# Keeping the small matmuls of side work together, in front of the products of the next step

## The chip, the core and the metric

The kernel runs on one core of a Trainium2 chip. The metric is the device time of one execution in microseconds (us). The engines are named as in the profile: PE is TensorE (PEld its weight loads), DVE is VectorE, ACT is ScalarE, POOL is GpSimd, and SP issues most of the DMAs.

## The reference

Sequence length T = 256, model width D = 1024, batch 1, float32. Two blocks follow each other, each with two layers. Cut to its core:

```
for l in range(2):                                   # first block
    h = rms_norm(x);  z = h @ w_in + b_in
    ya = dilated_mixture_attention(rope(aq), rope(ak), av)      # 8 heads of 64
    qk = silu(causal_short_conv(z[q, k]))                       # 4 taps
    hm = mlstm_chunkwise(mq, mk, mv, mi, mf)                    # 4 heads of 128
    x += (sig(ga) * (ya @ w_proj_att) + sig(gb) * (yb @ w_proj_mlstm)) @ w_out
    x += relu(rms_norm(x) @ w_ff1) ** 2 @ w_ff2                 # 4096 wide
x = rms_norm(x)
for l in range(2):                                   # second block
    x += 0.5 * rms_norm(swiglu(rms_norm(x)))                    # 2816 wide
    z = rms_norm(x) @ w_in
    branches = gmlp(uv), pool(pz), sparse_attention(q, k, v, index), conv(cz)   # 256 wide each
    y = sum(sigmoid(gate_n) * (branch_n @ w_branch[n]) for n in range(4))
    x += rms_norm(y @ w_out)
    x += 0.5 * rms_norm(swiglu(rms_norm(x)))
```

The gMLP mixes tokens with a causal 128x128 matrix per group. Pool takes window means of 2 to 16 tokens. Sparse attention lets each query see the 64 keys that an index score picks. Conv is a depthwise convolution of 31 taps.

## The kernel before

All large matrix products are made of three TensorE products: each operand is split into a high part and a low part, and high x high, high x low and low x high are added in PSUM. Weights are streamed once, about 1 MB a tile: SP loads a tile (RAWS = 3 raw buffers), ACT casts the high part (L214), DVE subtracts to get the low part (L223); five high and four low tiles are held.

The work is written as a list of steps (`prog`). A step is one function of one weight tile. The products of a step are `a_mm` (tokens on the output's partitions; L309, L310 and L313; 512 or 256 columns) and `w_mm` (features on partitions; L322 to L324; 256 columns; a `w_step` has 48 of them). The ten phases are mix, ff, mix, ff of the first block, then f1, mix, f2, f1, mix, f2 of the second. At the border of two phases (`seam`), the two halves of the tokens are staggered, so that the norm of one goes on under the products of the other.

Everything else in the mixing phases is **side work**: generators that are put on a list by `spawn`. After each step `tick` advances every generator on the list by one piece (up to its next `yield`). The pieces that issue TensorE work are `prep` (rotary embedding and transposes of q and k), `gates_chain` (the stabiliser of the mLSTM; L865 to L867), `attend` (L768, L792), `mlstm` (L880, L881, L897), `gmlp` (L1106), `pool` (L1126 to L1135), `conv`, `choose` (L1202, the index score), `sparse` (L1231, L1254), `go` and, once at the start, `toeplitz` (L419). Transposes are recorded at L327. `choose` is spawned by the step that computes the index queries and keys, whose results ACT first copies out (L1268, L1270, L1272).

The program text is only one input to the order on the engines. A scheduler at build time plays the program through and lets each engine take, among the instructions that are ready, the one of highest priority; the priority is the place in the program. `tick` runs each piece under `high_priority(urge)`, which sets its instructions' place back by `urge` and lets the numbering go on from before the block: the first instructions of the piece and the first of the next step then have the same place, and so on. Instructions of equal place alternate.

PSUM has two pools of four banks, `wk` (products of `w_mm`, norms) and `acc` (products of `a_mm` of 512 columns, side work). In `gates_chain` two heads share a bank, and dependencies are kept by bank:

```
b = self.acc([P, 2, T])
ex = self.slot([P, 2, 384])
for j in range(2):
    h = 2 * g + j
    nc.tensor.matmul(b[:, j, :], lhsT=..., rhs=mr, start=True, stop=True)                # L865
    nc.vector.scalar_tensor_tensor(out=ex[:, j, 0:T], in0=b[:, j, :], ...)               # L866
    nc.vector.scalar_tensor_tensor(out=ex[:, j, T:384], in0=b[:, j, P:T], ...)           # L867
```

L768 and L1231 use 64 rows of the array (a head of 64), L1202 uses 32 rows, the pool's matmuls write 64 columns, L865 uses 4 rows; L792, L880, L881, L897, L1106, L1254 and the transposes of 128x128 use all 128 rows.

Of the kernel before, what the change touches and what calls it, by code (L numbers as in the profile page):

```python
# [13 lines left out]
OP = mybir.AluOpType  # L14
AX = mybir.AxisListType

P = 128
T = 256
HALF = (slice(0, 512), slice(512, 1024))
D = 1024  # L20
EPS = 1e-6
# [73 lines left out]
class XT:  # L95
    """Activations with features on partitions, each as two float32r parts that sum to it."""

# [11 lines left out]
class XS:  # L109
    """The same for two chunks, both parts in one slot."""  # L110

# [14 lines left out]
class Net:  # L126
    def __init__(self, ctx, tc, a, out):
        self.tc, self.nc, self.a, self.out = tc, tc.nc, a, out
        self.sb = ctx.enter_context(tc.tile_pool(name="sb", bufs=1))
        self.ps = ctx.enter_context(tc.tile_pool(name="ps", bufs=4, space=bass.MemoryType.PSUM))  # L130
        self.dr = ctx.enter_context(tc.tile_pool(name="dr", bufs=1, space=bass.MemoryType.DRAM))
        self.stream = []
        self.prog = []
        self.side, self.urge, self.pace = [], {}, 1
        self.late = []

# [1 line left out]
    def slot(self, shape, dt=F32):  # L138
# [16 lines left out]

# [1 line left out]
    def weight(self, shape, *loads):  # L157
# [10 lines left out]

    def tick(self):
        for g in list(self.side):  # L170
            if g in self.side:
                try:
                    with self.tc.high_priority(self.urge.get(g, 0)):
                        next(g)
                except StopIteration:
                    self.side.remove(g)

# [77 lines left out]

# [1 line left out]
    def little(self, src, n):  # L257
        """At most 8 columns of a matrix with 1024 rows, as float32r parts."""
        raw = self.own("lraw", [P, 8, 8])
        self.dma(out=raw[:, :, 0:n], in_=src.rearrange("(k p) n -> p k n", p=P))  # L260
        return raw
# [5 lines left out]
    def little_mm(self, n):  # L267
        """Those columns of the projection, one on a partition; the products of the others that a
        stationary operand of 128 columns takes in are left."""
        nc = self.nc  # L270
        b = self.bank([P, T])
        for k in range(8):
            cs = slice(8 * k, 8 * k + P)
            xh, xl = self.xt.hi(k), self.xt.lo(k)
            nc.tensor.matmul(b, lhsT=self.lhi[:, cs], rhs=xh, start=k == 0, stop=False)
            nc.tensor.matmul(b, lhsT=self.lhi[:, cs], rhs=xl, start=False, stop=False)
            nc.tensor.matmul(b, lhsT=self.llo[:, cs], rhs=xh, start=False, stop=k == 7)
        r = self.own("lrow", [8, T])
        nc.scalar.copy(r[0:n, :], b[0:n, :])
        return r  # L280
# [16 lines left out]
    def a_mm(self, banks, x, k0, t, w, nk, first, last, width=512):  # L297
        """banks[h] += x[:, tokens t]^T @ w, for nk chunks of 128 rows."""
        nc = self.nc
        hi, lo = w  # L300
        ts = tok(t)
        groups = [[b] for b in enumerate(banks)] if last else [list(enumerate(banks))]
        for group in groups:
            for k in range(nk):
                xh, xl = x.hi(k0 + k, ts), x.lo(k0 + k, ts)
                start, stop = first and k == 0, last and k == nk - 1
                for h, b in group:
                    cs = slice(h * width, (h + 1) * width)
                    nc.tensor.matmul(b, lhsT=xh, rhs=hi[:, k, cs], start=start, stop=False)  # L309
                    nc.tensor.matmul(b, lhsT=xh, rhs=lo[:, k, cs], start=False, stop=False)  # L310
                for h, b in group:
                    cs = slice(h * width, (h + 1) * width)
                    nc.tensor.matmul(b, lhsT=xl, rhs=hi[:, k, cs], start=False, stop=stop)  # L313

    def w_mm(self, dst, x, w, c0, nk, k0=0):
        """dst = w[:, c0:c0+128]^T @ x, features on partitions."""
        nc = self.nc
        hi, lo = w
        cs = slice(c0, c0 + P)
        for k in range(nk):  # L320
            xh, xl = x.hi(k0 + k), x.lo(k0 + k)
            nc.tensor.matmul(dst, lhsT=hi[:, k, cs], rhs=xh, start=k == 0, stop=False)  # L322
            nc.tensor.matmul(dst, lhsT=hi[:, k, cs], rhs=xl, start=False, stop=False)  # L323
            nc.tensor.matmul(dst, lhsT=lo[:, k, cs], rhs=xh, start=False, stop=k == nk - 1)  # L324

# [3 lines left out]
    def rstd(self, ss, inv, n=1):  # L329
        """(ss * inv + EPS) ** -0.5"""  # L330
        nc = self.nc
        ms, r = self.tiny(n), self.tiny(n)
        nc.gpsimd.tensor_scalar(out=ms, in0=ss, scalar1=inv, scalar2=EPS, op0=OP.mult, op1=OP.add)
        nc.gpsimd.tensor_tensor(out=r, in0=ms, in1=self.mhalf[:, 0:n], op=OP.pow)
        return r

    def row(self, src, n):
        """A row of DRAM on all partitions."""
        s = self.slot([P, n])
        self.dma(out=s, in_=src.partition_broadcast(P))  # L340
        return s

# [1 line left out]
    def setup(self):  # L344
# [55 lines left out]
    def toeplitz(self):  # L400
        """rel_bias by distance for query rows 128.., with -1e30 after the diagonal."""
        nc, a = self.nc, self.a
# [6 lines left out]
        rows = self.slot([33, 4, P])  # L409
# [15 lines left out]

# [1 line left out]
    def rstd_halves(self, ss):  # L427
        """(mean of 1024 squares + EPS) ** -0.5 from the sums over both halves."""
        nc = self.nc
# [11 lines left out]
    def norm_pre(self, t, w, ss, out=None):  # L441
        """The norm of x[t] from its sums of squares; out: over x itself, else into a slot."""
        r = self.rstd_halves(ss)
# [22 lines left out]
    def post_residual(self, t, accs, w, half):  # L466
        """x += (0.5 *) rms_norm(acc) * w"""
        nc = self.nc
# [9 lines left out]
    def seam(self, ends, pre, starts, lead=0):  # L478
        """The end of one phase and the start of the next, the two halves of the tokens apart, so
        that the norm of one goes on under the products of the other.  # L480
        ends[t], starts[t]: steps of each half; pre(t) -> what turn(t) takes."""
        held = {}
# [34 lines left out]

# [1 line left out]
    def w_tile(self, src, c0, n=256):  # L519
        """Columns c0.. of a matrix with 1024 rows."""  # L520
        return self.weight([P, 8, n], (lambda r: r, src[:, c0 : c0 + n].rearrange("(k p) n -> p k n", p=P)))

    def a_tile(self, src, r0):
        """256 rows of a matrix with 1024 columns."""
        return self.weight([P, 2, D], (lambda r: r, src[r0 : r0 + 256, :].rearrange("(k p) n -> p k n", p=P)))

    def z_tile(self, src, c0, half):
        """512 rows, 512 columns."""
        return self.weight([P, 4, 512], (lambda r: r, src[half * 512 : half * 512 + 512, c0 : c0 + 512].rearrange("(k p) n -> p k n", p=P)))

    def z_group(self, tiles, done):
        """512 columns of the projection with tokens on partitions: steps for each half of the tokens."""
        accs = {}
# [31 lines left out]

# [1 line left out]
    def ff_plan(self, tag, w1, w2, kind, head):  # L567
        """The steps of a feed-forward phase: starts[t] and body and ends[t]."""
        nc = self.nc
# [106 lines left out]

# [1 line left out]
    def mix1_plan(self, l):  # L678
# [125 lines left out]
        def conv(c, b):  # L804
            """Two blocks of 128 channels: short convolution and twice the silu of it."""
            pt = st["pt"]
# [18 lines left out]
        def gates_chain(rows):  # L825
            """Stabiliser rows and columns from the input and forget gates."""
            yield
# [193 lines left out]

# [1 line left out]
    def mix2_plan(self, l):  # L1023
# [116 lines left out]
        def glu(ba, bg):  # L1140
            """Twice a * sigmoid(g), after 30 zeros; dw carries the half."""
            hb = st["hb"] = self.slot([P, 2, 30 + T])
# [48 lines left out]
        def choose():  # L1191
            """The mask of the 64 best keys of each query, 0 or -1e30."""
            qik, causal = st["qik"], self.const("causal")
# [70 lines left out]
        def body():  # L1264
            def qik(b):
                """The keys of the index at the partitions of each of its heads; its weights below them."""
                st["qik"] = self.half([P, 2, T])
# [81 lines left out]

# [1 line left out]
    def plan(self):  # L1351
# [134 lines left out]
```

## Time and profile before

| what | value |
|---|---|
| runs | 2034.19, 2036.45, 2040.32 us; median 2036.45 |
| span of the profiled execution | 2032.4 us |
| the median run above that span | 4.05 us |
| instructions on TensorE | 13544 matmuls, 13544 weight loads |
| busy: TensorE, DVE, ACT, POOL | 1993.8, 1215.2, 933.6, 77.3 us |

The profiled execution has no time of its own beside its span; it is set against the median of the runs. Times in rows are from the start of the span. A matmul's duration in the rows is longer than the distance to the next one, since matmuls are pipelined: distances are taken from start to start. A row with x8 stands for eight in succession of the same line and form. "[0.25 <-DVE half L1100]" is idle time of the engine in front of the row, and what ended it.

### The profile page before, as it was taken

Reading aid. Unit: us, or ns where it says so; the run is one execution under the profiler, and the core shown is the slowest. Engines: PE = TensorE matmul, PEld = TensorE weight load, DVE = VectorE, ACT = ScalarE, POOL = GpSimd, SP = SyncE. Lnnn points to the kernel's source line nnn. Section 1 sums busy time; section 2 is a strip of 40 time slices with the busy share of each in tenths; the row PEclk is TensorE's granted clock in tenths of the full one; section 3 lists DMA queues with packets and bytes.
Section 4 is the critical chain, followed back from the end, with each engine's and each line's share of the span. In section 5 each row is a group of like instructions: output and inputs, shape, how many; then the busy total and the mean of one; then the engine's idle time right before and its main releaser. Section 6 shows DMA issues by size and latency. Waiting matters only on the chain.

```text
span 2032.4 us, 32090 instructions
## 1 busy us (share of the span) xinstructions
PE 1993.8 (98%) x13544; PEld 1825.8 (90%) x13544; DVE 1215.2 (60%) x1730; ACT 933.6 (46%) x1380; POOL 77.3 (4%) x147
## 2 busy tenths in 40 slices
PE   7999999999999999999999999999999999999998
PEld 6889899887999998999889999998999889999997
DVE  6755755477566555544569666445544569666443
ACT  5554544354445444544444445444444444445442
POOL 0000000000000000000100000001000100001000
PEclk9999999999999999999999999999999999999999
DMA  8543565564445555556545556565556445546552
GB/s 277 183 153 132 168 206 187 187 207 151 141 155 169 185 193 179 197 186 210 160 133 163 166 168 206 186 208 165 186 185 212 148 125 162 170 166 201 187 193 74
DMA packets 252925, 357.23 MB, mean 176 GB/s; under 512 B 9399, under 2 KB 206188, under 8 KB 252780
## 3 DMA queue, kind: packets, MB, share of 16 engines
q1 hardware_dynamic: 252780, 355.17, 53.4%
q8 instruction: 106, 1.74, 0.4%
q14 instruction: 39, 0.32, 0.0%
HBM read 353.31 MB, written 1.84 MB: 175 GB/s over the span
## 4 chain that ended last, share of the span: by engine, by line
PE 90%; DMA 2%; DVE 2%; ACT 2%; POOL 2%; issue 1%; SPq 0%; DVEq 0%; POOLq 0%; ACTq 0%
PE wk L323 17%; PE wk L322 17%; PE wk L324 17%; PE acc L309 10%; PE acc L310 10%; PE acc L313 9%; PE wk L309 1%; PE wk L310 1%; PE wk L313 1%; ACT hi L214 1%; DMA raw<-in_ffn_w_gu_dram 1%; PE wk L327 1%; DMA raw<-in_w_in_dram 1%; PE acc L327 1%; POOL tiny L431 1%
## 5 line engine op out<-in xcount | busy, mean ns | idle before, releaser
L223 DVE TENSOR_TENSOR lo<-raw,hi 128x1024 fp32r<-128x1024 f32 (+1 forms) x646 | 767.8, 1217 | 448.8 <-issue 285.6
L214 ACT CAST hi<-raw 128x1024 fp32r<-128x1024 f32 (+1 forms) x646 | 660.7, 1046 | 801.8 <-PE wk L323 475.4
L322 PE MATMUL wk<-slot,hi 128*128 128x256 f32 x2880 | 824.1, 286 | 3.7 <-ACT slot L291 3.7
L323 PE MATMUL wk<-slot,hi 128*128 128x256 f32 x2880 | 823.6, 286 | 0.0
L324 PE MATMUL wk<-slot,lo 128*128 128x256 f32 x2880 | 822.8, 286 | 0.0
L322 PEld LDWEIGHTS wk<-slot,hi 128*128 128x128 f32 x2880 | 553.5, 192 | 10.8 <-ACT slot L291 4.2
L323 PEld LDWEIGHTS wk<-slot,hi 128*128 128x128 f32 x2880 | 553.7, 192 | 7.0 <-issue 3.3
L324 PEld LDWEIGHTS wk<-slot,lo 128*128 128x128 f32 x2880 | 553.8, 192 | 4.2 <-issue 3.3
L309 PE MATMUL acc<-hi,slot 128*128 128x512 f32 x960 | 379.6, 395 | 2.8 <-ACT slot L291 2.8
L310 PE MATMUL acc<-lo,slot 128*128 128x512 f32 x960 | 379.0, 395 | 0.0
L313 PE MATMUL acc<-hi,slot 128*128 128x512 f32 x960 | 324.8, 394 | 0.0
L309 PEld LDWEIGHTS acc<-hi,slot 128*128 128x128 f32 x960 | 181.4, 189 | 39.5 <-ACT slot L291 3.5
L313 PEld LDWEIGHTS acc<-hi,slot 128*128 128x128 f32 x960 | 180.8, 188 | 39.8 <-DVE slot L292 1.4
L310 PEld LDWEIGHTS acc<-lo,slot 128*128 128x128 f32 x960 | 181.1, 189 | 36.5 <-issue 0.7
L313 PE MATMUL wk<-hi,slot 128*128 128x256 f32 x352 | 100.6, 286 | 1.8 <-DVE slot L292 1.8
L309 PE MATMUL wk<-hi,slot 128*128 128x256 f32 x352 | 102.0, 290 | 0.0
L310 PE MATMUL wk<-lo,slot 128*128 128x256 f32 x352 | 100.7, 286 | 0.0
L634 DVE TENSOR_TENSOR slot<-wk,slot 128x512 f32<-128x512 f32 x36 | 24.9, 692 | 122.9 <-PE wk L324 122.9
L431 POOL TENSOR_SCALAR tiny<-tiny 128x1 f32<-128x1 f32 x34 | 28.0, 824 | 1332.5 <-ACT slot L438 1326.3
L313 PEld LDWEIGHTS wk<-hi,slot 128*128 128x128 f32 x352 | 68.0, 193 | 2.6 <-DVE slot L292 2.6
L309 PEld LDWEIGHTS wk<-hi,slot 128*128 128x128 f32 x352 | 68.0, 193 | 0.7 <-ACT slot L610 0.4
L310 PEld LDWEIGHTS wk<-lo,slot 128*128 128x128 f32 x352 | 68.1, 193 | 0.2
(241 smaller groups left out, 1217.3 us busy)
## 6 DMA issues: line engine op xcount, KB each, us to landing
raw<-in_w_in_dram SPq DMA_DIRECT2D x90, 1024.0 KB
raw<-in_ffn_w_gu_dram SPq DMA_DIRECT2D x88, 1024.0 KB
raw<-in_w_ff_dram SPq DMA_DIRECT2D x64, 1024.0 KB
raw<-in_ffn_w_down_dram SPq DMA_DIRECT2D x44, 1024.0 KB
raw<-in_w_out_dram SPq DMA_DIRECT2D x16, 1024.0 KB
raw<-in_w_branch_dram SPq DMA_DIRECT2D x8, 1024.0 KB
raw<-in_w_proj_att_dram SPq DMA_DIRECT2D x4, 1024.0 KB
raw<-in_w_proj_mlstm_dram SPq DMA_DIRECT2D x4, 1024.0 KB
```

Source lines behind the costliest of these rows:

```text
L214: nc.scalar.copy(his[j][:, p], raw[j][:, p])
L223: nc.vector.tensor_sub(lo[:, p], r[:, p], hi[:, p].bitcast(F32))
L309: nc.tensor.matmul(b, lhsT=xh, rhs=hi[:, k, cs], start=start, stop=False)
L310: nc.tensor.matmul(b, lhsT=xh, rhs=lo[:, k, cs], start=False, stop=False)
L313: nc.tensor.matmul(b, lhsT=xl, rhs=hi[:, k, cs], start=False, stop=stop)
L322: nc.tensor.matmul(dst, lhsT=hi[:, k, cs], rhs=xh, start=k == 0, stop=False)
L323: nc.tensor.matmul(dst, lhsT=hi[:, k, cs], rhs=xl, start=False, stop=False)
L324: nc.tensor.matmul(dst, lhsT=lo[:, k, cs], rhs=xh, start=False, stop=k == nk - 1)
L327: self.nc.tensor.transpose(dst, src, self.ident[: src.shape[0], : src.shape[0]])
L431: nc.gpsimd.tensor_scalar(out=m0, in0=ss[0], scalar1=1.0 / D, scalar2=EPS, op0=OP.mult, op1=OP.add)
L634: nc.vector.tensor_mul(r[:, 1], b, r[:, 0])
```

## The change

`tick` forgets the old fences and collects new ones: for each generator that it advances, the last TensorE instruction that the piece has traced. Every product of a step, through the new function `product`, is ordered behind all fences of the last tick. The order is one of issue on the same engine (`NoSync`): no semaphore and no instruction is added. So the matmuls and transposes of a piece can no longer alternate with products of the next step; they stand in front of them, and the products stand behind the piece even if the piece is not ready. Fences last until the next tick: steps that do not tick (`sides=False`) and those after them keep the last ones. Pieces that are completed by `finish` outside of a tick set no fence. Apart from this, only comments and descriptions were removed.

```
+BEHIND = mybir.DependencyInfo(mybir.DependencyClass.NoSync, mybir.DependencyReason.DATA)
...
     def tick(self):
+        self.fences = []
         for g in list(self.side):
             if g in self.side:
-                try:
-                    with self.tc.high_priority(self.urge.get(g, 0)):
-                        next(g)
-                except StopIteration:
-                    self.side.remove(g)
+                with self.burst():
+                    try:
+                        with self.tc.high_priority(self.urge.get(g, 0)):
+                            next(g)
+                    except StopIteration:
+                        self.side.remove(g)
+
+    @contextmanager
+    def burst(self):
+
+        traced = self.nc.cur_bb.bb.instructions
+        n = len(traced)
+        yield
+        mine = [i for i in self.nc.cur_bb.bb.instructions[n:] if i.engine == mybir.EngineType.PE]
+        if mine:
+            self.fences.append(mine[-1])
+
+    def product(self, *args, **kwargs):
+
+        i = self.nc.tensor.matmul(*args, **kwargs)
+        for f in self.fences:
+            self.tc.add_manual_dep(i.ins, f.name, BEHIND, reason="burst")
...
-                    nc.tensor.matmul(b, lhsT=xh, rhs=hi[:, k, cs], start=start, stop=False)
-                    nc.tensor.matmul(b, lhsT=xh, rhs=lo[:, k, cs], start=False, stop=False)
+                    self.product(b, lhsT=xh, rhs=hi[:, k, cs], start=start, stop=False)
+                    self.product(b, lhsT=xh, rhs=lo[:, k, cs], start=False, stop=False)
...
-                    nc.tensor.matmul(b, lhsT=xl, rhs=hi[:, k, cs], start=False, stop=stop)
+                    self.product(b, lhsT=xl, rhs=hi[:, k, cs], start=False, stop=stop)
...
-            nc.tensor.matmul(dst, lhsT=hi[:, k, cs], rhs=xh, start=k == 0, stop=False)
-            nc.tensor.matmul(dst, lhsT=hi[:, k, cs], rhs=xl, start=False, stop=False)
-            nc.tensor.matmul(dst, lhsT=lo[:, k, cs], rhs=xh, start=False, stop=k == nk - 1)
+            self.product(dst, lhsT=hi[:, k, cs], rhs=xh, start=k == 0, stop=False)
+            self.product(dst, lhsT=hi[:, k, cs], rhs=xl, start=False, stop=False)
+            self.product(dst, lhsT=lo[:, k, cs], rhs=xh, start=False, stop=k == nk - 1)
```

## Rows read from the trace of the kernel before

**Rows 1.** The page: busy time, share, count by engine; chain that ended last.

```profile
PE 1993.8 (98%) x13544; PEld 1825.8 (90%) x13544; DVE 1215.2 (60%) x1730; ACT 933.6 (46%) x1380; POOL 77.3 (4%) x147
...
PE 90%; DMA 2%; DVE 2%; ACT 2%; POOL 2%; issue 1%; SPq 0%; DVEq 0%; POOLq 0%; ACTq 0%
```

**Rows 2.** Timeline, PE, stage of L1231 with 256 columns: start, us, instruction.

```profile
1083.59 0.28 PE L324 MATMUL wk<-slot,lo 128*128 128x256 f32 x1
1083.80 0.70 PE L1231 MATMUL acc<-slot 64*128 64x256 f32 x2
...
1087.36 0.39 PE L323 MATMUL wk<-slot,hi 128*128 128x256 f32 x1
```

**Rows 3.** Timeline, PE, stage of L1231 with 128 columns.

```profile
1106.76 0.28 PE L324 MATMUL wk<-slot,lo 128*128 128x256 f32 x1
...
1109.69 0.39 PE L323 MATMUL wk<-slot,hi 128*128 128x256 f32 x1
```

**Rows 4.** Timeline, PE, start of choose in the first layer.

```profile
1043.74 0.47 PE L322 MATMUL wk<-slot,hi 128*128 128x256 f32 x1
...
1046.27 0.22 PE L327 MATMUL acc<-ident,lrow 4*128 4x4 f32 x1 [0.40 <-ACT lrow L1272]
...
1046.41 1.10 PE L1202 MATMUL acc<-half 32*128 32x256 f32 x5
1047.45 0.38 PE L322 MATMUL wk<-slot,hi 128*128 128x256 f32 x1
...
1048.42 0.69 PE L1202 MATMUL acc<-half 32*128 32x256 f32 x2
```

**Rows 5.** Timeline, PE, transposes of prep in the second layer.

```profile
444.54 1.06 PE L327 MATMUL acc<-ident,slot 128*128 128x128 f32 x8 [0.15 <-DVE slot L744]
445.36 0.36 PE L324 MATMUL wk<-slot,lo 128*128 128x256 f32 x1
```

**Rows 6.** Timeline, PE, pool in the first layer: before and after it.

```profile
1028.96 0.39 PE L313 MATMUL acc<-hi,slot 128*128 128x512 f32 x1
...
1039.12 0.39 PE L323 MATMUL wk<-slot,hi 128*128 128x256 f32 x1
```

**Rows 7.** Timeline, PE, a stage of L792: before and after it.

```profile
122.58 0.28 PE L324 MATMUL wk<-slot,lo 128*128 128x256 f32 x1
...
124.07 0.28 PE L323 MATMUL wk<-slot,hi 128*128 128x256 f32 x1
```

**Rows 8.** Timeline, PE, L865 in the first layer.

```profile
75.16 0.67 PE L865 MATMUL acc<-half,ident 4*128 4x256 f32 x2
...
80.30 0.69 PE L865 MATMUL acc<-half,ident 4*128 4x256 f32 x2
...
82.28 0.69 PE L865 MATMUL acc<-half,ident 4*128 4x256 f32 x2
```

**Rows 9.** Timeline, DVE, the readers of L865's bank in the first layer.

```profile
76.66 0.46 DVE L866 SCALAR_TENSOR_TENSOR slot<-acc,gu,table 128x256 f32<-128x256 f32 x1
...
79.49 0.33 DVE L867 SCALAR_TENSOR_TENSOR slot<-acc,gu,table 128x128 f32<-128x128 f32 x1
...
84.95 0.35 DVE L867 SCALAR_TENSOR_TENSOR slot<-acc,gu,table 128x128 f32<-128x128 f32 x1
```

**Rows 10.** Timeline, PE, gmlp's matmuls in the first layer.

```profile
1026.07 2.30 PE L1106 MATMUL acc<-half 128*128 128x64 f32 x16 [0.25 <-DVE half L1100]
```

**Rows 11.** Timeline, PE, toeplitz at the start.

```profile
40.57 1.70 PE L419 MATMUL wk<-slot 33*128 33x384 f32 x4 [0.42 <-PE acc L327]
```

**Rows 12.** Windows: stretch, us, busy (count) of PE, PEld, DVE, ACT, POOL, PEclk, DMA, GB/s.

```profile
183.00:186.00 3.00, 1.48 (x9) 1.48 (x10) 2.40 (x4) 2.41 (x5) 0.00 (x0) 0.86 0.24 20
186.00:189.00 3.00, 3.00 (x18) 3.00 (x18) 0.00 (x0) 0.00 (x0) 0.00 (x0) 0.57 0.80 329
...
1649.00:1651.00 2.00, 2.00 (x12) 2.00 (x11) 0.00 (x0) 0.15 (x1) 0.00 (x0) 0.50 0.00 0
```

**Rows 13.** Timeline, ACT, the cast in front of the copies for choose.

```profile
1043.14 1.05 ACT L214 CAST hi<-raw 128x1024 fp32r<-128x1024 f32 x1 [3.33 <-PE wk L323]
```

## What I predicted, and how

> **What bounds the kernel now.** The page's busy times come first, then its chain that ended last [rows 1]. TensorE is busy in 98% of the span and makes 90% of the chain; DVE is busy in 60% and ACT in 46%. So a microsecond saved on TensorE is a microsecond of the run, and so is one in which TensorE waits, because no other engine holds a reserve of work that it could bring forward. Waits off TensorE cost nothing. The change touches only the order on TensorE, so two things are read from its timeline: what alternation of side matmuls with products costs now (a gain if it goes), and which side matmuls wait for DVE, ACT or DMA while products run in front of them (a loss, since products may no longer run there).
>
> The unit is the start-to-start time of undisturbed products: 0.120 us for 256 columns (in the timeline, L322 to L324 follow each other at 0.12) and 0.227 us for 512. What a stretch takes beyond its products at that spacing is the price of the side work in it.
>
> **Gain: switches of shape.** In the 256-column stage of L1231 four pairs of passes alternate with five products [rows 2]: 1087.36 - 1083.59 = 3.77, less 5 x 0.12 = 0.60, leaves 3.17 us for 8 passes. A pass of 256 columns in a group takes 0.21 us: five L1202 passes stand between 1046.41 and 1047.45 [rows 4]. So 8 x 0.21 = 1.68 is work and 1.49 is four changes in and out, 0.37 each. In the 128-column stage [rows 3] it is 1109.69 - 1106.76 = 2.93, less 5 x 0.12, so 2.33; a grouped pass of 128 columns takes (445.36 - 444.54)/8 = 0.10 [rows 5], taken as 0.11 with its load, so 0.88 is work and 1.45 is four changes, 0.36 each. Grouped, one change is left and three are saved: 3 x 0.36 = 1.08 us a stage.
>
> - Second block's mixing, per layer: both L1231 stages and the first-half stage of L1202, the same pattern of four pairs: 3 x 1.08. Two layers: 6.5.
> - First block's mixing, L768, per layer four stages, of which one already stands together: 3 x 1.08. Two layers: 6.5.
> - Pool, L1126 to L1129: from 1028.96 to 1039.12 [rows 6] 10.16 us with 17 products (16 x 0.12 + 0.23 = 2.15), so 8.01 for 16 wide passes, 16 passes of 16 columns and 4 transposes that fell between. Grouped: 16 x 0.11 + 16 x 0.08 + 4 x 0.11 + 0.36 = 3.84. Gain 4.2, two layers 8.4. The bounds are 3.1 (the narrow passes no cheaper than wide ones) and 4.8 a layer.
> - Shapes of the full array gain nothing. L792 alternates as four pairs in 124.07 - 122.58 = 1.49 [rows 7]; less 5 x 0.12, 0.89 is left for 8 passes, and 8 grouped at 0.11 are 0.88. The same holds for L897, L1254 and the transposes. Taken as 0; at 0.07 a stage the other way, 18 stages would lose 1.2.
>
> The Trainium skill, "TensorE: Matmul & The Clock Gate", section "LDWEIGHTS (loading the stationary operand)", puts the load of 128 columns at about 107 ns, and its "Step-by-step" section lets the next load run under the current matmul. It speaks against grouping here: a 64-column pass is too short to hide a load, a product isn't. By it, L792 grouped would cost 8 x 0.107 = 0.86, and the sum would not change.
>
> Sum of gains 6.5 + 6.5 + 8.4 = **21.4**, between 16 and 29.
>
> **Loss: waits that products fill now.** Each product now waits behind the last side matmul of the last tick, and whatever that one waits for stops TensorE.
>
> - L865 in the chain of the gates. The matmul of the second head writes the bank that DVE's L866 and L867 read for the first head. First group of heads: the first matmul ends at 75.83, the second starts at 80.30 [rows 8], and products fill what is between. DVE ran L866 at 76.66, then other pieces' work, and L867 from 79.49 to 79.82 [rows 9]. With the change TensorE stands from 75.83 to about 79.9: 4.1. Second group: from 82.97 [rows 8] to L867's end at 85.30 [rows 9], 2.3 as DVE is ordered now; no less than about 1.0 (the two DVE instructions, 0.48 + 0.35, and the hop). What DVE did in between is work of the same tick, which 4.1 us of standstill lets it do earlier; I take the middle, 1.7. Two layers: 2 x (4.1 + 1.7) = 11.6, between 4 and 12.8. Behind it in TensorE's queue stand 24 products of the step, and behind those the bank that the step's `done` reads: all of it is later by the same time.
> - The start of choose. The turn of the index weights needs L1272 on ACT and came at 1046.27 with 15 products ahead of it since 1043.74; the fourth head's L1202 waited for a bank, with 5 products from 1047.45 to 1048.42 [rows 4]. These 20 products move behind: 20 x 0.12 = 2.4, less one change of shape, 0.36. Two layers: 4.1, at most 4.8.
> - L1106 of gmlp waits for L1100 on DVE (ready at 1026.07 [rows 10]; already 0.25 idle). Some 8 products of its step stand in front of it, 8 x 0.227 = 1.8. Two layers: 3.6; nothing, if its chain came first.
> - Transposes of prep, second layer, wait for L744 [rows 5]; eleven products in front: 1.3.
> - The start: toeplitz's L419 [rows 11] becomes a fence for the first keys' products. Before, only its own operands held it up; now the products of the next two steps stand behind it too. No row shows that order, so I take one such gap, 0.42 [rows 11], once for each of two steps, and the seam's own wait: 1.0, between -1 (it leaves the way of later work) and 5 (a whole step).
> - The clock. At the seam by 184 TensorE worked 1.48 of 3 us. After it the granted clock was 0.57 for 3 us, between the levels of 1.2 and 2.4 GHz, with 18 matmuls [rows 12]: 3.0 - 18 x 0.12 = 0.84 lost, with 0.2 in the window before about 1.0 (1.5 if all of it went with the clock). Four new gaps are as long (the first of L865 and that of choose, in two layers): 4.2. On the other side the second layer's alternating pool drew a clock of 0.50 without any gap: 12 matmuls in 2 us [rows 12], 0.56 lost, and the stretch is 6.8 us long: 1.9 may come back. Net 2.3.
>
> The Trainium skill, "TensorE: Matmul & The Clock Gate", section "Why this matters for your kernels", says that idle gaps between bursts of matmuls send the clock back to its lower level. The seam by 184 agrees (0.57).
>
> Waits of conv, attend and mlstm cost nothing: their DVE and ACT work is done within the step that hides it (5.8 us of 48 products), so the next tick's matmuls find it ready. If that cover went, each would cost what its DVE piece is late. The added order itself is on one engine and adds no instruction and no DMA; SP's and POOL's queues keep theirs.
>
> Sum of losses 11.6 + 4.1 + 3.6 + 1.3 + 1.0 + 2.3 = **23.9**, between 12 and 37.
>
> **Net** 23.9 - 21.4 = +2.5. The profiled span is 2032.4; the median of the runs is 2036.45, 4.05 above it, which I keep. 2032.4 + 2.5 + 4.05 = 2038.95, so **2039.0 us**: no change that can be measured.
>
> **Rivals.**
>
> *A, slower: the clock.* Place: every new gap, not only the long ones. There are some ten (four of L865, two of choose, two of gmlp, prep, the start). For it: the clock fell after one stretch half idle, 1.48 of 3 us busy, and in the pool with no gap at all. Against it: short gaps stand here already, and after the one of 0.40 the grouped passes took no more than 0.21 [rows 4]. At 1.5 each, 15 in place of 4.2: +10.8, so 2049.8. It decides from seven such gaps on.
>
> *B, faster: the chains come first.* The order on DVE and ACT is chosen when the kernel is built, by priority and by what is ready. If the fence leads to L866 and L867 being run one behind the other, the waits of L865 are 1.0 each, 4 in place of 11.6 (-7.6), and two gaps are too short for the clock (-2.1); if L1268 to L1272 pass the 1.05 us cast on ACT [rows 13], choose gains 2 x 1.05. Together -11.8: 2027.2. For it: DVE is 60% busy, so the four microseconds of L865 are a matter of order alone. Against it: nothing in the change alters a priority on DVE or ACT, and in the row before the other pieces went first, in both layers alike.
>
> *C, no effect:* the order was already mostly as asked. Against it stand the alternating rows [rows 2, 3, 6]; then 2036.4.
>
> **How the numbers follow.** Forecast (2034 to 2044 as its own range) 0.42, A 0.28, B 0.27, C 0.03. A change of 0.3%, 6.1 us, is about what a measurement here can tell: the band is 2030.3 to 2042.6. Faster: 0.21 of B and 0.04 from gains at their upper end, 0.25. Slower: A's 0.26 and 0.12 of the forecast whose waits reach their upper bound, 0.38. The same: 0.37. The range runs from B to a little above A: 2027 to 2051.
>
> **What would show it.** Right: L1126 to L1129 in one block of under 4.5 us; L768, L1231 and L1202 with eight passes in a row; TensorE idle before the second L865, put down to L867, of about 4 us; idle before the turn of the index weights of over 2 us; products' spacing unchanged elsewhere. Wrong: if the idle at L865 is under 1.5 (B); if PEclk falls behind short gaps (A); if the pool block takes over 6 us, the price of a switch was mis-sized; if side matmuls still stand singly between products (C). A new long wait at the start would come from toeplitz.

## The result, and the profile after

The changed kernel takes 2050.4 us (median of 4 runs, 2049.09 to 2051.02) against 2035.32 us before (median of 4, 2031.99 to 2040.32). The ratio is 1.0076, interval 1.0059 to 1.0094: slower by 15 us. The forecast was 2039.0, no measurable change, with a range from 2027 to 2051. The loss is clear of the noise, which the forecast did not expect, and the time lies at the upper end of the range, on the side of rival A.

In the lines below, all products stand at L194, and the other lines have moved by 18: L865 is L883, L867 is L885, L327 is L345, L419 is L437, L1106 is L1124, L1126 to L1129 are L1144 to L1147, L1202 is L1220, L1231 is L1249.

The page of the changed kernel: span, busy time by engine, and the chain that ended last.

```profile
span 2048.6 us, 32097 instructions
...
PE 1977.3 (97%) x13544; PEld 1822.4 (89%) x13544; DVE 1213.7 (59%) x1730; ACT 932.6 (46%) x1380; POOL 77.7 (4%) x147
...
PE 84%; DVE 7%; DMA 3%; ACT 3%; POOL 1%; issue 1%; SPq 0%; DVEq 0%; POOLq 0%; ACTq 0%
```

TensorE is busy for 16.5 us less than in [rows 1], with the same instructions, and yet the span is 16.2 us longer. So work became cheaper and waits were added, of some 33 us. The chain says the same: TensorE's share fell from 90% to 84%, DVE's rose from 2% to 7%.

The waits of TensorE in the changed kernel: who waits for whom, us in total, times, longest. The row for L464 is the norms between the phases, where 12.8 us stood before.

```profile
PE wk L345 <- DVE slot L464: 12.7, 8, 7.7
PE wk L437 <- DVE slot L428: 12.5, 1, 12.5
PE acc L883 <- DVE slot L885: 9.7, 4, 4.0
PE acc L345 <- ACT lrow L1290: 4.4, 2, 2.2
...
PE acc L345 <- DVE slot L762: 2.8, 2, 1.5
...
PE acc L1124 <- DVE half L1118: 2.2, 2, 1.1
PE acc L345 <- ACT slot L1256: 2.0, 2, 1.0
```

Five of these rows are waits that the prediction named (toeplitz, gates, choose, prep, gmlp). Gates, choose and prep have about the length it gave and gmlp half of it; the second row, toeplitz, has twelve times the term. The last row, the transposes of sparse behind the exponentials on ACT, it did not name.

Both traces have the same 12,576 products, so the start of the n-th product in one, less that in the other, is how far the changed kernel is behind. Each is counted from its own first product, which the changed kernel starts 0.28 us earlier. Worked out from the two timelines:

```
products       before, us          behind at the end   change   what lies there
0-240          12.4 to 69.1        14.7                +14.7    start, toeplitz
240-336        69.1 to 90.1        23.6                 +8.9    gates, layer 1
336-864        90.1 to 191.9       17.5                 -6.1    attend, mlstm, seam
864-2496       191.9 to 462.9      18.4                 +0.9    prep, layer 2
2496-2592      462.9 to 483.8      27.0                 +8.6    gates, layer 2
2592-3120      483.8 to 584.2      23.9                 -3.1    attend, mlstm, seam
3120-5904      584.2 to 1020.6     24.2                 +0.3
5904-5952      1020.6 to 1040.2    19.4                 -4.8    pool
5952-6000      1040.2 to 1049.6    23.9                 +4.5    choose, first piece
6000-6864      1049.6 to 1167.9    20.6                 -3.3    choose, sparse, conv
6864-9936      1167.9 to 1629.1    20.9                 +0.3
9936-9984      1629.1 to 1650.3    16.1                 -4.9    pool
9984-10032     1650.3 to 1660.9    19.8                 +3.8    choose, first piece
10032-12576    1660.9 to the end   16.5                 -3.4    choose, sparse, conv
```

The change does both of the things that the prediction set against each other. Grouping gains in every stretch in which scores and windows are computed, and five stretches lose 40.5 us: the start, the gates twice, the first piece of choose twice.

The start: a window of the kernel before (columns as in [rows 12]), then of the changed kernel the timelines of PE, SP's queue and DVE, and windows:

```profile
30.00:40.00 10.00, 9.46 (x46) 7.59 (x44) 8.60 (x13) 6.57 (x7) 0.00 (x0) 1.00 0.79 241
```

```profile
25.18 0.40 PE L194 MATMUL acc<-hi,slot 128*128 128x512 f32 x1
38.11 1.62 PE L437 MATMUL wk<-slot 33*128 33x384 f32 x2 [12.54 <-DVE slot L428]
```

```profile
18.32 13.79 SPq L220 DMA_DIRECT2D raw<-in_w_in_dram  x4
32.17 0.52 SPq L423 DMA_DIRECT2D slot<-in_buckets_dram  x1
32.78 0.33 SPq L426 DMA_DIRECT2D rb<-in_rel_bias_dram  x1
```

```profile
37.59 0.42 DVE L428 COPY slot<-rb 33x512 f32<-33x512 f32 x1 [3.60 <-DMA rb<-in_rel_bias_dram]
```

```profile
33.00:36.00 3.00, 0.00 (x0) 0.00 (x0) 0.99 (x1) 1.06 (x2) 0.00 (x0) 0.50 0.97 311
36.00:39.00 3.00, 0.89 (x2) 0.61 (x3) 0.42 (x1) 0.00 (x0) 0.00 (x0) 0.50 1.10 344
39.00:42.00 3.00, 3.00 (x7) 1.42 (x6) 0.00 (x0) 0.96 (x2) 0.00 (x0) 0.50 0.71 126
```

TensorE stands still for 12.54 us in front of toeplitz's first matmul. That matmul needs L428 on DVE, which needs a load of 0.5 KB, which stands in SP's queue behind four weight tiles whose buffers have to come free: they take the queue from 18.32 to 32.11. DVE then waits for the load until 37.59. In the kernel before, products ran all through this time and L419 came at 40.57 [rows 11], when everything was there. Behind the wait the clock is at its lower level, 7 matmuls in 3 us; in the kernel before it is so a little later as well (last section), so most of the 14.7 is the wait itself.

The gates, timelines of PE and DVE, and windows:

```profile
89.57 0.67 PE L883 MATMUL acc<-half,ident 4*128 4x256 f32 x2
94.28 1.21 PE L883 MATMUL acc<-half,ident 4*128 4x256 f32 x2 [4.04 <-DVE slot L885]
...
104.85 0.69 PE L883 MATMUL acc<-half,ident 4*128 4x256 f32 x2 [0.48 <-DVE slot L885]
```

```profile
91.07 0.46 DVE L884 SCALAR_TENSOR_TENSOR slot<-acc,gu,table 128x256 f32<-128x256 f32 x1
...
93.90 0.33 DVE L885 SCALAR_TENSOR_TENSOR slot<-acc,gu,table 128x128 f32<-128x128 f32 x1
```

```profile
92.00:95.00 3.00, 0.72 (x2) 0.50 (x2) 3.00 (x10) 0.74 (x1) 0.64 (x1) 0.63 0.00 0
95.00:98.00 3.00, 3.00 (x8) 2.09 (x7) 2.90 (x7) 1.36 (x3) 0.11 (x1) 0.50 0.17 27
98.00:101.00 3.00, 3.00 (x11) 2.36 (x11) 2.93 (x8) 0.73 (x2) 0.00 (x0) 0.73 0.93 323
...
107.00:110.00 3.00, 3.00 (x9) 2.38 (x8) 0.00 (x0) 0.45 (x1) 0.00 (x0) 0.53 0.97 290
```

The wait is the one that was read from [rows 8, 9]: between L884 and L885 DVE ran the same other work as before, and 4.04 us stand where 4.1 were forecast. What was too small is what follows: in three windows, nine microseconds, the mean granted clock is 0.63, 0.50 and 0.73, and it falls once more (0.53) behind the short wait of the second group.

The gain, timeline of PE: the two stages of [rows 2, 3], the second scores of choose, and the end of the pool block, which began at 1054.11.

```profile
1105.47 0.28 PE L194 MATMUL wk<-slot,lo 128*128 128x256 f32 x1
1105.68 1.14 PE L1249 MATMUL acc<-slot 64*128 64x256 f32 x8
1106.75 0.51 PE L194 MATMUL wk<-slot,hi 128*128 128x256 f32 x2
...
1128.66 0.28 PE L194 MATMUL wk<-slot,lo 128*128 128x256 f32 x1
1128.87 0.72 PE L1249 MATMUL acc<-slot 64*128 64x128 f32 x8
1129.53 0.50 PE L194 MATMUL wk<-slot,hi 128*128 128x256 f32 x2
...
1087.79 0.50 PE L1220 MATMUL acc<-half 32*128 32x128 f32 x8
1088.22 0.50 PE L194 MATMUL wk<-slot,hi 128*128 128x256 f32 x2
...
1056.35 0.50 PE L194 MATMUL wk<-slot,hi 128*128 128x256 f32 x2
```

The eight passes stand in a row, as the diff says. The 256-column stage costs 1106.75 - 1105.47 - 0.12 = 1.16 in place of 3.17, so it gains 2.0 and not 1.08; the 128-column stage 0.75 in place of 2.33, a gain of 1.6. Eight passes of L1220 take 1088.22 - 1087.79 = 0.43 us. The pool is one block of 2.24 us, and the four transposes in front of it stand together too.

### The profile page after: what moved, and what is told of

Read it like the earlier page. It is cut to its first block, busy times and chain, and to the rows that moved or that the text cites. A ratio compares the mean times of both kernels' runs of the same rounds, so it can differ in the third digit from the quotient of the medians.

```text
span 2048.6 us, 32097 instructions
## 1 busy us (share of the span) xinstructions
PE 1977.3 (97%) x13544; PEld 1822.4 (89%) x13544; DVE 1213.7 (59%) x1730; ACT 932.6 (46%) x1380; POOL 77.7 (4%) x147
## 4 chain that ended last, share of the span: by engine, by line
PE 84%; DVE 7%; DMA 3%; ACT 3%; POOL 1%; issue 1%; SPq 0%; DVEq 0%; POOLq 0%; ACTq 0%
PE wk L194 51%; PE acc L194 28%; DVE lo L243 3%; ACT hi L234 1%; DMA raw<-in_ffn_w_gu_dram 1%; DMA raw<-in_w_in_dram 1%; PE wk L345 1%; DVE half L1176 1%; PE acc L345 1%; POOL tiny L449 1%; DVE slot L464 1%; DVE half L835 1%; DMA raw<-in_w_ff_dram 1%; PE acc L810 0%; PE acc L786 0%
## 5 line engine op out<-in xcount | busy, mean ns | idle before, releaser
L194 PE MATMUL wk<-slot,hi 128*128 128x256 f32 x5760 | 1051.0, 285 | 3.7 <-ACT slot L311 3.7
L234 ACT CAST hi<-raw 128x1024 fp32r<-128x1024 f32 (+1 forms) x646 | 661.6, 1046 | 846.9 <-PE wk L194 503.1
L194 PEld LDWEIGHTS wk<-slot,hi 128*128 128x128 f32 x5760 | 905.1, 193 | 12.2 <-ACT slot L311 4.2
L194 PE MATMUL wk<-slot,lo 128*128 128x256 f32 x2880 | 816.8, 284 | 0.0
L194 PE MATMUL acc<-hi,slot 128*128 128x512 f32 x1920 | 624.1, 398 | 2.7 <-ACT slot L311 2.7
L194 PEld LDWEIGHTS wk<-slot,lo 128*128 128x128 f32 x2880 | 554.6, 193 | 0.0
L194 PEld LDWEIGHTS acc<-hi,slot 128*128 128x128 f32 x1920 | 366.8, 191 | 82.5 <-ACT slot L311 3.3
L194 PE MATMUL acc<-lo,slot 128*128 128x512 f32 x960 | 381.3, 397 | 0.6 <-DVE lo L243 0.6
L194 PEld LDWEIGHTS acc<-lo,slot 128*128 128x128 f32 x960 | 183.5, 191 | 36.9 <-DVE lo L243 1.0
L194 PE MATMUL wk<-hi,slot 128*128 128x256 f32 x704 | 134.2, 288 | 1.9 <-DVE slot L312 1.9
L194 PEld LDWEIGHTS wk<-hi,slot 128*128 128x128 f32 x704 | 112.5, 193 | 3.4 <-DVE slot L312 2.7
L194 PE MATMUL wk<-lo,slot 128*128 128x256 f32 x352 | 100.7, 286 | 0.0
L194 PEld LDWEIGHTS wk<-lo,slot 128*128 128x128 f32 x352 | 68.1, 194 | 0.2
L345 PE MATMUL wk<-ident,slot 128*128 128x128 f32 x216 | 41.3, 283 | 19.8 <-DVE slot L464 12.7
L1176 DVE SCALAR_TENSOR_TENSOR half<-slot,prmT,half 128x256 f32<-128x256 f32 x120 | 54.4, 480 | 1.1
L311 ACT CAST slot<-wk 128x512 fp32r<-128x512 f32 (+1 forms) x68 | 32.1, 498 | 49.8 <-PE wk L345 49.3
L312 DVE TENSOR_TENSOR slot<-slot 128x512 fp32r<-128x512 f32 x62 | 42.6, 688 | 17.9 <-ACT slot L311 17.9
L345 PEld LDWEIGHTS wk<-ident,slot 128*128 128x128 f32 x216 | 27.2, 144 | 29.0 <-issue 9.5
```

What stands on the lines that cost most here:

```text
L194: i = self.nc.tensor.matmul(*args, **kwargs)
L234: nc.scalar.copy(his[j][:, p], raw[j][:, p])
L311: nc.scalar.copy(hi, src)
L312: nc.vector.tensor_sub(lo, src, hi.bitcast(F32))
L345: self.nc.tensor.transpose(dst, src, self.ident[: src.shape[0], : src.shape[0]])
L1176: nc.vector.scalar_tensor_tensor(out=cv[:, c, :], in0=hb[:, c, k : k + T], scalar=w, in1=cv[:, c, :], op0=OP.mult, op1=OP.add)
```

## The experiments

The theory after the result (W): the loss is the sum of waits at a few places, each worth its length and the lower clock behind it, and grouping by itself is worth what the forecast said or more. Rivals: a wait that is taken away comes back behind the next late piece (M); it is the fences as such that cost (Q, S); grouping gains nothing by itself (G). All kernels are the changed one with the edit shown; times are medians, ratios are to the kernel before, run on the same chip with a median of 2034.1 to 2035.9 us.

**Toeplitz sets no fence.**

```
-        if mine:
+        if mine and g.__name__ != "toeplitz":
             self.fences.append(mine[-1])
```

> The change, but toeplitz sets no fence; all other pieces do. In the trace of the change TensorE stands still for 12.54 us in front of toeplitz's first matmul, then runs at the lower clock; by the start of product 240, on the way into the gates' chain, it is 14.7 us behind the kernel before. Theory W (the loss is the sum of waits at a few places, each worth its length and the slow clock after it): 14.7 us come back, 2050.4 - 14.7 = 2035.7, between 2033 and 2039, no wait of TensorE over 2 us before 90 us, the waits of the gates' chain as they are. Rival M (a wait that is taken away at the start comes back behind the next late piece, because weights and banks are late there too): at most half comes back, 2043 or more.

Measured: 2043.77 us, ratio 1.0045 (1.0030 to 1.0061). Only 6.6 of the 14.7 us came back. Timeline of PE, and windows:

```profile
34.80 0.39 PE L194 MATMUL acc<-hi,slot 128*128 128x512 f32 x1
38.45 1.54 PE L345 MATMUL acc<-ident,slot 128*128 128x128 f32 x6 [3.26 <-DVE slot L762]
```

```profile
39.00:42.00 3.00, 3.00 (x8) 1.75 (x7) 3.00 (x4) 0.39 (x2) 0.00 (x0) 0.50 0.51 113
42.00:45.00 3.00, 3.00 (x6) 1.56 (x5) 0.72 (x2) 1.89 (x4) 0.00 (x0) 0.50 0.90 351
45.00:48.00 3.00, 3.00 (x8) 2.07 (x7) 0.29 (x2) 1.42 (x2) 0.00 (x0) 0.50 0.49 172
```

Rival M was right here: the next late piece is prep, whose transposes wait 3.26 us for the rotary embedding on DVE, and the clock is down for twelve microseconds. The two waits had overlapped, which the run without both fences (below) bears out.

**Toeplitz's loads come early, all fences stay.** Its two loads, the memset and the copy L428 move into the first step, in front of the second weight tile.

```
                     self.first_loads(1)
+                    self.toeplitz_loads()
                     self.dma(out=self.x[1], in_=a["x"][0, tok(1), :])
```

> The change with all its fences; toeplitz's two loads and the DVE copy are issued before the second weight tile instead of behind the sixth. Theory W (its matmul is late because its load of 0.5 KB stands behind four weight tiles in SP's queue): the wait of 12.54 us falls under 1.5 us and the time is that without toeplitz's fence plus up to 1.5, 2036 to 2038.5. Rival Q (the fence itself is the cost: TensorE has to take the small matmuls at a bad place, whatever they wait for): the time stays above 2045.

Measured: 2033.25 us, ratio 0.9991 (0.9977 to 1.0004), better than either expected. No wait in front of toeplitz is left in its trace. The first products come 4.6 us later: the first weights land as before (the cast L234 starts at 9.73, before at 9.69), but on ACT the squares of the first norm now stand behind three of these casts, at 11.29 instead of 4.57. This is made up by product 144; the granted clock is 1.00 in all windows from 12 to 51, which is worth some 3 us there and need not come from the edit (last section). Rival Q falls: with the same fences, the change costs nothing once this one load is early.

**The same without toeplitz's and prep's fences.**

```
+        if mine and g.__name__ not in ("toeplitz", "prep"):
```

> The change with neither toeplitz nor prep setting a fence. Without toeplitz's fence alone 2043.77 us were measured: prep's transposes then wait 3.26 us for DVE at 35, and the clock is at 0.50 from 39 to 50, together 7.8 us behind the kernel before. Theory W2 (each late piece at the start costs its own wait and the slow clock after it; prep is the second one): the 7.8 us and some 1.2 of prep in the second layer come back, 2043.8 - 9.0 = 2034.8, between 2032 and 2037. Rival M2 (the loss of the start moves on to a third piece): 2040 or more.

Measured: 2031.95 us, ratio 0.9984 (0.9974 to 0.9994). The time is at the lower edge of what W expected (2032 to 2037), and M2 falls: there is no third piece. Its trace is even 3.0 us ahead of the kernel before at product 240; the clock there is low for a shorter time (last section).

**Each head of the gates in a bank of its own**, without toeplitz's fence:

```
-                b = self.acc([P, 2, T])
...
                 for j in range(2):
...
+                    b = self.acc([P, T])
```

> The change without toeplitz's fence, and in the chain of the gates each head's broadcast gets a PSUM bank of its own. In the trace of the change TensorE waits 9.7 us there in the two layers, and 8.9 us a layer are lost around it. Theory W (the second head waits because DVE still reads the first head's half of the same bank): the four waits are gone, and with them the low clock behind them; 10 to 16 us less than without toeplitz's fence alone, 2020 to 2026. Rival D (DVE is late for its other work anyway, so the next piece waits for it instead): less than 4 us gained, 2032 or more.

Measured: 2023.91 us, ratio 0.9943 (0.9923 to 0.9962), 19.9 below the 2043.77 of the same kernel with the shared bank; 10 to 16 were expected. The waits for L885 are gone, and the stretch of the gates goes from 8.9 us behind to 0.8 ahead, in both layers. D falls. The wait was for the other half of the same bank, and the slow clock behind it was worth about as much as the wait itself.

**Fences of the gates alone.**

```
+        if mine and g.__name__ == "gates_chain":
```

> The kernel before with fences of gates_chain alone. Theory W2: the 8.9 us a layer that the change loses around it come alone: 2034.1 + 17.8 = 2051.9, between 2048 and 2054, with TensorE waiting 9 to 10 us for DVE in front of the second head and the clock under 0.7 behind the first of these waits in each layer. Rival S (the loss there belongs to all the fenced pieces of these steps, conv and mlstm among them): under 10 us more, below 2045. The prediction had 5.8 us a layer, and 2.1 of the clock for both: 2047.8.

Measured: 2050.07 us, ratio 1.0071 (1.0051 to 1.0091). Its waits on TensorE:

```profile
PE acc L883 <- DVE slot L885: 9.0, 4, 4.0
```

One piece of side work costs nearly as much as the whole change; 9.0 us of wait cost 14.2 in the run, and in the trace the two stretches of the gates lose 7.7 and 7.5. S falls.

**Fences of pool alone.**

```
+        if mine and g.__name__ == "pool":
```

> The kernel before with fences of pool alone. Theory W2: the 4.8 us a layer that the change gains around it come alone, with a little from the clock in the second layer: 2034.1 - 10 = 2024, between 2021 and 2027. The prediction had 4.2 a layer and 1.9 of the clock: 2023.8. Rival G (the gain in the change comes from what else is grouped there, not from pool): under 4 us, 2030 or more.

Measured: 2023.02 us, ratio 0.9931 (0.9914 to 0.9949). The two stretches of pool gain 4.8 and 6.2 us, the second with the clock that the alternation had drawn down [rows 12]. G falls for pool.

**Fences only behind pieces that change the shape of the array and are ready.** A piece sets the flag itself.

```
-        if mine:
+        if mine and self.hold:
...
+                    self.hold = True          # scores of attend; the same for sparse, pool
...
+                self.hold = t == 0            # choose: not in its first piece
```

> Fences only behind the pieces that change the shape of the array and are ready: the scores of attend and of sparse, the second scores of choose, and the windows of pool. Everything else may alternate with products, as before. Theory W (grouping is worth what the spacing shows, and only waits cost): the gain that the prediction added up, 21.4 us, comes alone: 2035.3 - 21.4 = 2013.9, between 2010 and 2019. Rival G (an alternating matmul costs little, because the product between hides it, so a switch was priced too high): under 10 us of gain, 2025 or more.

Measured: 2006.44 us, ratio 0.9863 (0.9843 to 0.9882): 27.7 below, where 21.4 were expected (2010 to 2019). G falls for the scores too. In its list of waits only those of the kernel before are left, and 2.5 us for the transposes of sparse.

**The same pieces by priority, without any fence**: their loops stand under `high_priority(64)`. These hold the first scores of choose as well, and the instructions on DVE and ACT that read the scores.

> No fences at all; instead the same four kinds of pieces that were fenced in the run of 2006.44 us (scores of attend and sparse, scores of choose, windows of pool) are traced at a priority 64 places ahead, so that they win over products when they are ready, while products may run in front of them when they are not. Theory W2 (what counts is that the matmuls stand together; the fence is one way to it): 2004 to 2011. Rival F (at build time they become ready one after the other, so products slip in between and the switches stay): 2020 or more.

Measured: 2009.32 us, ratio 0.9868 (0.9851 to 0.9886). As good within the intervals. F falls: what counts is that the matmuls stand together, and products may still run in front when a piece is late. Here the wait for the transposes of sparse does not appear; whether this is the missing fence or the priority of the readers is not shown.

**One late piece fenced again**, the first of choose:

```
-                self.hold = t == 0
+                self.hold = True
```

> The kernel of 2006.44 us (fences behind the scores of attend and sparse, the second scores of choose and the windows of pool), with one more fence: behind the first piece of choose, whose turn of the index weights waits for ACT. In the trace of the change TensorE waits 2.18 us and once more 0.4 us there, and falls 4.5 and 3.8 us behind in the two layers. Theory W2 (a wait costs its length and the slow clock that follows it, and the cases add up): 2006.4 + 8.3 = 2014.7, between 2012 and 2017. The prediction had 2.05 a layer for the wait and 1.0 for the clock: 2012.5. Rival S (the loss there belongs to several fenced pieces, gmlp and conv among them): under 4 us more, below 2010.5.

Measured: 2012.67 us, ratio 0.9897 (0.9879 to 0.9915): 6.2 above 2006.44, close to the forecast's price (6.1) and under that of the trace (8.3). S falls here too, since it wanted under 4. Windows:

```profile
1028.00:1031.00 3.00, 1.12 (x7) 0.66 (x5) 2.36 (x2) 2.77 (x7) 0.40 (x2) 1.00 0.03 8
1031.00:1034.00 3.00, 2.19 (x9) 1.29 (x10) 1.32 (x3) 2.93 (x8) 0.00 (x0) 0.67 0.46 99
1034.00:1037.00 3.00, 3.00 (x13) 2.40 (x12) 2.25 (x7) 0.38 (x1) 0.00 (x0) 0.50 0.78 270
```

A wait of 2.19 us, then the clock: the stretch is 4.3 and 4.6 us longer in the two layers. The whole traces differ by 5.5, because elsewhere, without an edit, the clock falls at other places.

**The gates grouped with banks of their own, added to the kernel of 2006.44 us.**

```
-                b = self.acc([P, 2, T])
+                self.hold = True
                 ex = self.slot([P, 2, 384])
                 for j in range(2):
+                    b = self.acc([P, T])
```

> The kernel of 2006.44 us with each head's broadcast of the gates in a bank of its own, and fences behind these pieces too. Theory W2 (with nothing to wait for, grouping the four-row matmuls saves one change of shape of some 0.36 us for each of four pieces): 2006.4 - 1.4 = 2005.0, at most 2007. Rival D (DVE still holds something back there): over 2009, with waits of TensorE in front of the second head.

Measured: 2000.75 us, ratio 0.9843 (0.9826 to 0.9860), the fastest of all. The gates gain 0.8 a layer, as expected; what the trace has beyond that lies in stretches without an edit, above all 3.3 us at the start, where the clock was not down. How much of it repeats from run to run stays open.

## Why the prediction was right and wrong

The sum was +2.5, no change that can be measured. The spans of the two profiles differ by 16.2, and by 16.5 from the first product on. By step:

- **The start, forecast 1.0 (between -1 and 5), measured 14.7.** This step failed. It said that "the products of the next two steps" stand behind toeplitz, and priced that by the gap of 0.42 in front of L419 at 40.57 [rows 11]. But 0.42 is the wait that was left after products had run until everything was ready. With a fence, the piece stands at its place in the program, and that place is in front of the products that ran from 25 on. The price is the distance from there to the moment when its operands are ready (38.01), and the way back from L428 to its load and the queue of SP was there to be read. The run with early loads shows the cause, the run without the fence that prep, not priced at all in the first layer, stood hidden behind it.
- **The gates, forecast 11.6 and half of 4.2 for the clock, measured 17.5.** The mechanism, the place and the first wait (4.1 forecast, 4.04 measured) were right. The second wait was 0.5 in one layer and 1.1 in the other rather than 1.7. The size of the clock was wrong: 1.0 for each long gap, and nothing for the short ones. Of some 8.8 us a layer, 4.9 are waits and 4 are the clock.
- **The first piece of choose, forecast 4.1 and the other half of the clock, measured 8.3**, for the same reason; the wait itself came as forecast (2.04 forecast, 2.18 measured in each layer).
- **Prep in the second layer, forecast 1.3, measured 1.3; gmlp, forecast 3.6, measured 1.7** (2.2 of waits where 0.5 stood before).
- **A wait that has no term: sparse's transposes.** The forecast put the waits of conv, attend and mlstm at nothing, because their work is "done within the step that hides it", and did not speak of sparse. For the exponentials of sparse it does not hold, and 1.0 us a layer is waited for.
- **The clock that was to come back at the second pool, forecast 1.9: nothing in the changed kernel.** The second pool's stretch gains 4.9 like the first, since the clock falls there behind gmlp's wait. With pool alone it gains 6.2 against 4.8.
- **The gain, forecast 21.4, measured 27.7 when it stands alone.** The number of switches was right, but a pass in a group was priced at 0.21 and 0.11, and it takes 1.07 / 8 = 0.13 for L1249 with 256 columns and 0.43 / 8 = 0.05 for L1220 with 128. The 0.21 was read from [rows 4], from five passes that stand together but start 0.11 to 0.32 us apart; in the changed kernel two of L1249 or four of L1220 start within 0.02. Some 3 of the 27.7 are the clock and not the passes: 1.4 at the second pool, and 1.5 at the seam by 184, which the run with pool alone gains as well. (The lower bound of the pool's gain, 3.1, does not follow from the forecast's own figures: with the narrow passes at 0.11 it is 3.7.)
- **Full-array shapes gain nothing, no instruction is added, products keep their spacing: right.**

Of the rivals, A had part of the mechanism, and its sign came: the clock fell behind some short gaps too.

```profile
1656.00:1659.00 3.00, 3.00 (x9) 2.33 (x9) 2.89 (x10) 0.27 (x1) 0.00 (x0) 0.51 0.43 151
```

This window stands behind gmlp's wait of 1.10 in the second layer; the granted clock is 0.53 behind the gates' wait of 0.48 (above) and 0.56 behind that of 1.12 in the other layer. With the four long waits these are the seven low stretches that A wanted. Behind gmlp's 1.10 in the first layer and prep's 1.47 the clock stays at 1.00, so the length of a gap alone did not decide it. B fails where it counted: in the first group of heads L885 came behind the same other work as in [rows 9]. In the second group L884 and L885 followed each other, as B had it. C fails.

So two errors of opposite sign: some 6 us too little gain, and some 20 too little loss at the start and from the clock. That the time came inside the range, by 0.6 us, is luck: with the gain as forecast it would have been outside. It is luck too that A's 2049.8 is so near, since the start was no part of A.

## What to carry to other kernels

Grouping small matmuls and making products wait for them are two things, and only the first is worth having: order a group ahead by priority, or fence only pieces whose operands are ready at that place. The price of a fence is read from the place where the piece stands in the program to the moment when its last operand is ready, back through every queue, and not from the wait that the old order had left. To a wait on the engine that bounds the kernel, the lower clock behind it is to be added: here some 2 to 4 us behind the long waits of choose and of the gates, and some 2 behind short ones where it fell.

## What the hardware showed that was not expected

Small passes on different strips of the array ran at the same time once they stood together. L1220 uses 32 rows, four heads on four strips: eight passes of 128 columns in 0.43 us, about half of what eight passes of the full array take (0.82 in [rows 5]). Four of them start at once. A narrow window of the timeline has them:

```profile
1087.79 0.39 PE L1220 MATMUL acc<-half 32*128 32x128 f32 x4
```

In the kernel before, they alternated with products:

```profile
1064.02 0.28 PE L322 MATMUL wk<-slot,hi 128*128 128x256 f32 x1
1064.23 0.48 PE L1202 MATMUL acc<-half 32*128 32x128 f32 x2
...
1067.18 0.39 PE L323 MATMUL wk<-slot,hi 128*128 128x256 f32 x1
```

That is 3.16 us, less seven products at 0.12: 2.32 us for eight, 0.29 each. The Trainium skill, "TensorE: Matmul & The Clock Gate", section "Part 3: Packing small matmuls — row/col tiling", says that tiles in different row groups overlap; the trace agrees, and the forecast had left it out.

The clock is not set by the kernel alone. At the start the kernel before and the last experiment have the same instructions and the same short gaps (0.54 and 0.42 us). Windows of the kernel before, then of the experiment:

```profile
43.00:46.00 3.00, 3.00 (x9) 1.74 (x9) 1.95 (x8) 2.40 (x4) 0.00 (x0) 0.50 0.85 335
```

```profile
43.00:46.00 3.00, 3.00 (x26) 2.84 (x25) 3.00 (x10) 2.32 (x4) 0.00 (x0) 1.00 1.02 396
```

The granted clock is 0.50 in one and 1.00 in the other, and it is worth 3.3 us by product 240. The run with pool alone has 1.00 in this window too; the runs of 2006.44, 2009.32 and 2012.67 us and the one with the gates alone have 0.50. So a difference of that size between two profiles, in a stretch that no edit touched, is not an effect of the edit.
